# A decoder layer on one core: first weights ahead of the first activations, batched squares, an earlier first norm, full-height gate rows and a split memory scaling

## The chip, the cores and the metric

The kernel runs on one core of a Trainium2 chip. A core has five engines, each with its own in-order instruction stream: TensorE (PE, matrix multiply; its weight loads are shown apart as PEld), VectorE (DVE), ScalarE (ACT), GpSimd (POOL) and SyncE (SP), which here only issues DMA transfers from main memory to on-chip memory. Engines wait for one another through semaphores, so a waiting instruction holds everything behind it on its engine. Matmul results go to PSUM, of which the kernel uses eight banks: four for the large products (named mm) and four for everything else (named ax).

The metric is the device time of one execution in microseconds, from the runs' own times. Over three runs the kernel before took 1468.85, 1471.32 and 1471.49 us, a median of 1471.32.

## The reference, cut to what matters

One inference step of one trunk layer. The prompt of 256 tokens and 8 sample tokens go through the same weights, so activations are 264 columns wide; the model width is 2048.

```python
def layer(x, ...):
    xn = rmsnorm(x, g_mix)
    z = xn @ w_in                       # all group inputs from one projection
    xr, conv_new = causal_conv(z[..., OFF_RGX:OFF_RGG], conv_buf, conv_w, conv_b)
    ...                                 # RG-LRU: gates from block_diag(xr), then a scan
    y_rg = rmsnorm(h_rg * jax.nn.gelu(z[..., OFF_RGG:OFF_Q]), g_rg_out)
    ...                                 # q, k, v; gate rows logi, logf (4 heads)
    h_ml, C_new, n_new, m_new = mlstm(q, k, v, logi, logf, C0, n0, m0)
    y_ml = rmsnorm(h_ml, g_ml_out) * jax.nn.sigmoid(z[..., OFF_O:OFF_I])
    x = x + jnp.concatenate([y_rg, y_ml], axis=-1) @ w_out
    xq = rmsnorm(x, g_xa) @ w_xa_q
    ...                                 # cross attention over 256 memory tokens
    x = x + o @ w_xa_o
    xf = rmsnorm(x, g_ffn)
    x = x + (jax.nn.silu(xf @ w_ffn_gate) * (xf @ w_ffn_up)) @ w_ffn_down

def mem_kv(mem, g_mem, w_k, w_v):
    mn = rmsnorm(mem, g_mem)            # memory keys and values
    ...
```

All inputs and weights are float32. The final result is one more RMSNorm of x.

## The kernel before, in words

Activations are kept with channels on the 128 partitions and tokens in the columns: 16 chunks of 128 channels, each 264 wide. A float32 product is made of three single-pass products (`mm3`): every operand is split into a high part, rounded to the matmul type, and a low part, the remainder; high times high, high times low and low times high are accumulated in one PSUM bank.

The layer's weights are a list of `steps`, called blocks below and numbered from 0. A block is a weight column group of 128 outputs: 16 chunks times three products, 48 matmuls of 128x264. Blocks 0 to 7 make the RG-LRU input, 8 the gate rows of the mLSTM, 9 to 16 its q and k, 17 to 24 its v, 25 to 32 the RG-LRU's output gate (rgg), 33 to 40 the mLSTM's output gate (o), 41 to 56 w_out; the query, memory, attention output and feed-forward blocks follow. Blocks 0 to 3 are different: their weights come in quarters of the channels, and the four outputs are accumulated side by side in banks ax, ax, ax and mm (`pe_first`), so that the first matmuls need only the first chunks of the input.

Each block's weights come as two halves of 128x1024 float32 (buffers `raw`, five of them, filled by SP's DMA queue). `split_half` makes the two parts of a half: ACT copies it to the matmul type (`w<-raw`), and DVE subtracts that from the raw half (`w<-raw,w`). The split weights have four buffers `w`, two blocks' worth: a half's ACT copy waits until PE has done the last matmul that reads the buffer's old contents. So on ACT and DVE the splits of a block stand in the queue at a fixed distance ahead of PE, and what stands behind a split on either engine waits with it.

The order of instructions on the five engines is set when the program is built, by a scheduler that places them by its own estimate of when each could start, under priorities the code gives (`tc.high_priority`, `tc.issue_after`, `in_order`). Work beside the main stream is written as generators (`side`) that are advanced between blocks; `yield STEP` in one moves its next piece to a later block.

The first RMSNorm's factor (`rstd`) is not applied before the products but to their results. The input's squares are summed over chunks (`sumsq` into `acc_x`), PE sums that over partitions (three matmuls against `ones`, the token sums), DVE makes the inverse square root in a chain of small instructions (tiles `c`), PE spreads it over partitions (`ident` against `c`), and only then can the results of blocks 0 and on be evacuated from their banks: "evacuation" is the DVE instruction that multiplies a bank by `rstd` and frees it.

`ml_gates` turns block 8's rows into the mLSTM's gates, on 4 partitions, one for each head: it ends in nine small products that spread the rows over the partitions (tile ax to `bcs`, `gcol`, `emc`). `rg_gen` is the RG-LRU: sigmoids, then a run of exponentials and square roots on ACT. `ml_heads` is the mLSTM by heads, and `ml_norm` its norm with 24 one-column matmuls against `ones`. `mem_gen` normalises the memory: sixteen chunks, each multiplied by its factor and then split.

Of the kernel before, what the change touches and what calls it, by code (L numbers as in the profile page):

```python
# [80 lines left out]
def layer_kernel(ctx: ExitStack, tc, xT, memT, vec, wrg, w_in, w_out, w_q, w_k, w_v, w_o,  # L81
# [120 lines left out]
    def split_first(i, h):  # L202
# [9 lines left out]
        splits[i, h] = (wh, wl)  # L212

    def wrows(w, i):

        w = w[:, WO: WO + 8 * N].rearrange("p (c n) -> p c n", n=N)
        return w[:, :, 0: P], w[:, :, P: 2 * P]
# [97 lines left out]

    warm(12)
    onesr = const.tile([P, P], F32R, name="onesr")
# [276 lines left out]
    def evac_if(ps):  # L594
        R = Arr(7)
        ml["R"] = R
        li, u, a, b = (R(j)[0:4] for j in range(4))
        act.activation(halves(a), unturn(ps[64:68, :N]), AF.Copy)
# [14 lines left out]
    def ml_gates():  # L613
# [32 lines left out]
        for h in range(H):  # L646
            pe.matmul(ps[:, h * 16: h * 16 + 16], ident[0:4, h: h + 1].to_broadcast([4, P]), x16,
                      start=True, stop=True)
        i4 = ident[0:4, 0:4]
        for j in range(2):  # L650
            pe.transpose(ps[:, 64 + 4 * j: 68 + 4 * j], g[:, j * P: j * P + P], i4)
        for j, w0 in enumerate(WIN):
            pe.transpose(ps[:, 72 + 4 * j: 76 + 4 * j], b[:, w0: w0 + P], i4)
        act.activation(bcs, ps[:, 0:64].rearrange("p (h j) -> p h j", j=16), AF.Copy)
# [30 lines left out]
    def ml_prompt():  # L685
# [11 lines left out]
        R = ml["R"]  # L697
        M = R(6)[0:4, :T]
        for h in range(H):
            sel = ident[0:4, h: h + 1].to_broadcast([4, P])  # L700
            bc = bank("ax")
# [186 lines left out]
    def proj(src, rhs, evac, cols=2048, n=N, need=()):  # L888

        def f(i):  # L890
            ps = bank()
            w = W(i)
            nch = cols // P
            for c in range(nch):
                mm3(ps[:, :n], w(c), rhs(c), c == 0, c == nch - 1)
            return ps
        steps.append((src, cols, f, evac, need))
# [49 lines left out]
    def norm_x():  # L947
        yield from rstd_from(acc_x, rstd, D)
# [29 lines left out]
    def mem_gen():  # L978
# [14 lines left out]
        for c in range(KC):  # L993
            x = raw(c)
            dve.tensor_mul(x, x, r)
            m = rm(c)
            split(m[:, :T], m[:, T:], x, V("g_mem", c))
            yield 0.7

    def ry(c):  # L1000
# [304 lines left out]

    load_x(sp, 0, 1)
    for c in range(4):
        load_first(0, c)
    for i in range(1, 3):
        for c in range(0, 4, 2):  # L1310
# [3 lines left out]
        if i == 1:  # L1314
            sp.dma_start(vecs[:, 16:], vec[:, 16:])
    with tc.high_priority(), in_order():
        act.dma_start(vecs[:, 0:16], vec[:, 0:16])
        load_x(act, 1, 2)
        load_x(act, 2, 4)
        act.activation(warm_act, ones[:, 0:1], AF.Square)  # L1320
        split_half(0, 0)
        split_half(0, 1)

    pend = []
    for i, (src, cols, pef, evf, need) in enumerate(steps):
        if i > 1:
            load_piece(i + LD - 1)
        if i == 5:
            finish(lambda: fn.done)
            st["rg"] = side(rg_gen(), 0)  # L1330
        for q in need:
            if q in st:
                finish(lambda: st[q].done)
        if i != 4:
            with tc.high_priority(300):
# [6 lines left out]
        if i + LS < len(steps) and steps[i + LS][1] > 1024:  # L1342
            split_half(i + LS, 1)
        ps = pef(i)
        if 1 <= i < 4:
            with tc.issue_after(st["split"].ins):
                for c in range(4 * i if i > 1 else 0, 4 * i + 4):
                    sumsq(acc_x, xres[:, c, :], c == 0)
        if i == 3:
            fn = side(norm_x(), -1)  # L1350
        if evf is not None:
# [126 lines left out]
```

## Time and profile before

| what | value |
|---|---|
| median of three runs | 1471.32 us |
| the profiled execution's own time | 1470.12 us |
| its span, first to last instruction | 1468.0 us |
| PE busy in the span | 1447.7 us (99%) |
| DVE busy | 1054.0 us (72%) |
| ACT busy | 783.7 us (53%) |
| POOL busy | 125.7 us (9%) |
| mean granted TensorE clock | 0.994 |
| moved by DMA | 326.01 MB, 222 GB/s on average |

The table's profile is one execution. Its span is 2.1 us shorter than its own time, and its time is 1.2 us below the median. PE works for 99% of the span, so only its idle gaps and the instructions on it are to be won or lost; the groups' table gives each group's busy time, the mean time of one instruction, and the idle time of the engine just before them with the engine that ended it. A row's matmul ends are modelled: a matmul is shown with 0.28 us, although the next starts 0.11 us after it, so rows that follow each other overlap.

### The profile page before, as it was taken

How to read it: one execution, taken by the hardware profiler on the slowest of the kernel's cores; microseconds unless marked ns; L12 is line 12 of the kernel's file. 1: busy time of each engine (PE TensorE's matmuls, PEld its weight loads, DVE VectorE, ACT ScalarE, POOL GpSimd, SP SyncE). 2: the span in 40 equal slices, each digit the busy share in tenths (PEclk: the TensorE clock that was granted, in tenths of full speed). 3: DMA queues.
4: the chain of work that ended last, by engine and by line, in shares of the span. 5: the costliest groups of instructions: out<-in, count | busy, mean ns of one | idle time of the engine just before them, and what ended most of it. 6: DMA issues, size and time to landing. Idle time of an engine off the chain costs nothing.

```text
span 1468.0 us, 30204 instructions
## 1 busy us (share of the span) xinstructions
PE 1447.7 (99%) x12098; PEld 1423.3 (97%) x12098; DVE 1054.0 (72%) x2050; ACT 783.7 (53%) x1257; POOL 125.7 (9%) x190
## 2 busy tenths in 40 slices
PE   9999999999999999999999999999999999999997
PEld 9998899999999999999999999999999999999997
DVE  7986988798699999986666656555565655556564
ACT  7574775675455666665554444434444443444463
POOL 0001210000124344320000000000000000000000
PEclk9999999999999999999999999999999999999999
DMA  9555986556799979855555555555555555555563
GB/s 294 205 173 173 299 297 235 178 184 220 258 339 334 345 276 348 346 205 184 194 190 195 199 191 199 194 194 197 192 199 193 197 198 191 198 194 198 172 189 115
DMA packets 99756, 326.01 MB, mean 222 GB/s; under 512 B 10944, under 2 KB 19824, under 8 KB 99616
## 3 DMA queue, kind: packets, MB, share of 16 engines
q1 hardware_dynamic: 83472, 269.57, 53.8%
q0 software_dynamic: 15136, 53.16, 10.2%
q8 instruction: 94, 1.54, 0.4%
q10 hardware_dynamic: 1008, 1.36, 0.3%
q14 instruction: 46, 0.38, 0.1%
HBM read 312.78 MB, written 11.28 MB: 221 GB/s over the span
## 4 chain that ended last, share of the span: by engine, by line
PE 68%; DVE 1%; issue 0%; ACT 0%; POOL 0%; DVEq 0%; POOLq 0%; ACTq 0%
PE mm L60 65%; PE ax L60 2%; DVE B L60 0%; DVE w L60 0%; DVE dw L60 0%; POOL ds L1054 0%; ACT w L60 0%; DVE c L60 0%; ACT dw L60 0%; ACT ds L60 0%; DVE osm L60 0%; DVEq L1455 0%; ACT t L60 0%; DVE xres L60 0%; ACT c L60 0%
## 5 line engine op out<-in xcount | busy, mean ns | idle before, releaser
L60 PE MATMUL mm<-B,w 128*128 128x264 f32 (+1 forms) x10960 | 1285.7, 280 | 7.5 <-DVE w L60 3.6
L60 PEld LDWEIGHTS mm<-B,w 128*128 128x128 f32 x10960 | 1264.5, 190 | 15.7 <-DVE w L60 4.6
L60 DVE TENSOR_TENSOR w<-raw,w 128x1024 fp32r<-128x1024 f32 (+1 forms) x522 | 626.0, 1201 | 309.8 <-ACT w L60 309.1
L60 ACT ACTIVATE w<-raw 128x1024 fp32r<-128x1024 f32 (+1 forms) x522 | 535.7, 1028 | 539.5 <-PE mm L60 364.8
L60 PE MATMUL mm<-w,B 128*128 128x512 f32 x384 | 86.5, 380 | 0.0
L60 PEld LDWEIGHTS mm<-w,B 128*128 128x128 f32 x384 | 70.8, 190 | 9.3
L1370 POOL TENSOR_TENSOR B<-B,rstd 128x264 f32<-128x264 f32 x4 | 2.8, 743 | 803.7 <-ACT rstd L60 803.7
L60 DVE TENSOR_TENSOR t<-mm,rstd 128x264 f32<-128x264 f32 x104 | 44.9, 433 | 29.4 <-PE mm L60 29.4
L60 DVE SCALAR_TENSOR_TENSOR B<-B,dw 128x256 f32<-128x256 f32 x128 | 53.7, 474 | 2.9 <-ACT dw L60 2.7
L60 DVE TENSOR_TENSOR xres<-xres,mm 128x264 f32<-128x264 f32 (+1 forms) x81 | 34.4, 425 | 28.2 <-PE mm L60 28.1
L60 PE MATMUL ax<-B,B 128*128 128x256 f32 (+3 forms) x288 | 47.0, 304 | 1.8 <-DVE B L60 1.8
L60 DVE SCALAR_TENSOR_TENSOR dw<-B,qsm,dw 128x256 f32<-128x256 f32 x96 | 48.1, 509 | 0.7
L1054 POOL TENSOR_TENSOR ds<-dw,ds 128x256 fp32r<-128x256 f32 x32 | 35.9, 1122 | 106.0 <-ACT ds L60 105.9
L60 PEld LDWEIGHTS ax<-B,B 128*128 128x128 f32 x288 | 39.5, 191 | 5.3 <-DVE B L60 2.4
L60 ACT ACTIVATE B<-xres,vecs 128x264 fp32r<-128x264 f32 (+1 forms) x64 | 32.1, 501 | 2.5 <-DVE xres L60 2.0
L60 ACT ACTIVATE t<-xres 128x264 f32<-128x264 f32 (+1 forms) x61 | 23.9, 408 | 15.9 <-DVE xres L60 15.9
L1043 POOL DMA_DIRECT2D B<-kcT x32 | 17.3, 542 | 136.7 <-DVE B L60 123.6
L60 ACT ACTIVATE dw<-B,qsm 128x256 f32<-128x256 f32 x32 | 16.2, 507 | 21.5 <-issue 10.3
L60 ACT ACTIVATE t<-t 128x264 f32<-128x264 f32 (+1 forms) x61 | 24.8, 407 | 2.6 <-DVE t L60 2.6
L60 DVE TENSOR_TENSOR acc_x<-acc_x,t 128x264 f32<-128x264 f32 x59 | 25.3, 429 | 1.0 <-ACT t L60 0.5
L60 ACT ACTIVATE t<-B,B 128x128 f32<-128x128 f32 x64 | 21.6, 389 | 8.2 <-DMA B<-scr 8.2
L60 DVE SCALAR_TENSOR_TENSOR B<-xres,vecs,B 128x264 fp32r<-128x264 f32 x48 | 23.6, 491 | 3.1 <-ACT B L60 3.1
(152 smaller groups left out, 674.5 us busy)
## 6 DMA issues: line engine op xcount, KB each, us to landing
raw<-w_gu SPq DMA_DIRECT2D x176, 512.0 KB, 4.0
raw<-w_d SPq DMA_DIRECT2D x80, 512.0 KB, 4.3
raw<-w_in SPq DMA_DIRECT2D x74, 512.0 KB, 4.8
raw<-w_out SPq DMA_DIRECT2D x32, 512.0 KB, 4.3
B<-kcT POOLq DMA_DIRECT2D x32, 512.0 KB, 8.3
raw<-w_q SPq DMA_DIRECT2D x32, 512.0 KB, 4.2
B<-vcT POOLq DMA_DIRECT2D x32, 512.0 KB, 9.8
raw<-w_k SPq DMA_DIRECT2D x32, 512.0 KB, 5.4
```

Of the source, the lines that this page charges most:

```text
L60: return f(*a, **k)
L1043: pool_e.dma_start(kc, kcT[h, b])
L1054: pool_e.tensor_sub(ws[:, 1], acc, ws[:, 0].bitcast(F32))
L1370: e.tensor_mul(st["y"](c), st["y"](c), r)
```

## The change

The change has five parts.

Head: SP's first transfer is the first quarter of block 0's weights instead of the first input chunk; that chunk is issued by ACT ahead of the first vectors, and the other three of the first four by SP between the weights. The warm-up matmuls against `ones` go from 12 to 8 (each is two instructions in the profile).

Squares: the sixteen squares of single chunks are gone. After block 3, `first_squares` squares four chunks at a time on ACT (1056 columns), and DVE adds the four together and folds the sum to 264 columns.

First norm: the token sums are run inside block 5, after its first 8 chunks, and the spread inside block 6, after its first 4; PE's order is held as written from block 4 to block 6. The results of blocks 0 to 5 are handed to evacuation after that.

Gate rows: the two 4-row tiles that the small products read are cleared to 128 partitions, and the products are made over all 128, the five transposes as plain products with the identity.

Memory: the scaling of the memory chunks moves to a later block after every second chunk.

```diff
+    def first_squares():
+
+        a, b = (B([P, BW])[:, 0: 4 * N] for _ in range(2))
+        x = lambda q: xres[:, 4 * q: 4 * q + 4, :].rearrange("p c n -> p (c n)")
+        act.activation(a, x(0), AF.Square)
+        for q in range(1, 4):
+            act.activation(b, x(q), AF.Square)
+            dve.tensor_add(a, a, b)
+        dve.tensor_add(a[:, 0: 2 * N], a[:, 0: 2 * N], a[:, 2 * N:])
+        dve.tensor_add(acc_x, a[:, 0: N], a[:, N: 2 * N])
...
-    warm(12)
+    warm(8)
...
         ml["R"] = R
+        for q in range(2):
+            pool_e.memset(R.tile(q), 0.0)
...
         for h in range(H):
-            pe.matmul(ps[:, h * 16: h * 16 + 16], ident[0:4, h: h + 1].to_broadcast([4, P]), x16,
+            pe.matmul(ps[:, h * 16: h * 16 + 16], ident[:, h: h + 1].to_broadcast([P, P]), R(2)[:, 0:16],
                       start=True, stop=True)
-        i4 = ident[0:4, 0:4]
-        for j in range(2):
-            pe.transpose(ps[:, 64 + 4 * j: 68 + 4 * j], g[:, j * P: j * P + P], i4)
-        for j, w0 in enumerate(WIN):
-            pe.transpose(ps[:, 72 + 4 * j: 76 + 4 * j], b[:, w0: w0 + P], i4)
+        for o, x, at in ((64, R(5), WIN[:2]), (72, R(4), WIN)):
+            for j, w0 in enumerate(at):
+                pe.matmul(ps[:, o + 4 * j: o + 4 * j + 4], x[:, w0: w0 + P], ident[:, 0:4], start=True, stop=True)
...
-        M = R(6)[0:4, :T]
+        M = R(6)[:, :T]
         for h in range(H):
-            sel = ident[0:4, h: h + 1].to_broadcast([4, P])
+            sel = ident[:, h: h + 1].to_broadcast([P, P])
...
             for c in range(nch):
+                if (i, c) in ((5, 8), (6, 4)):
+                    with tc.high_priority():
+                        st["rstd_x"].run(lambda: True)
                 mm3(ps[:, :n], w(c), rhs(c), c == 0, c == nch - 1)
...
             split(m[:, :T], m[:, T:], x, V("g_mem", c))
             yield 0.7
+            if c % 2:
+                yield STEP
...
-    load_x(sp, 0, 1)
     for c in range(4):
         load_first(0, c)
+        if c == 0:
+            load_x(sp, 1, 2)
+        elif c == 1:
+            load_x(sp, 2, 4)
...
     with tc.high_priority(), in_order():
+        load_x(act, 0, 1)
         act.dma_start(vecs[:, 0:16], vec[:, 0:16])
-        load_x(act, 1, 2)
-        load_x(act, 2, 4)
...
+    kept = ExitStack()
...
-        if i == 5:
-            finish(lambda: fn.done)
+        if i == 6:
             st["rg"] = side(rg_gen(), 0)
...
-        if i != 4:
+        if not 4 <= i < 7:
...
+        if i == 4:
+            kept.enter_context(tc.manual_schedule(engines={mybir.EngineType.PE}))
         ps = pef(i)
-        if 1 <= i < 4:
-            with tc.issue_after(st["split"].ins):
-                for c in range(4 * i if i > 1 else 0, 4 * i + 4):
-                    sumsq(acc_x, xres[:, c, :], c == 0)
+        if i == 6:
+            kept.close()
         if i == 3:
-            fn = side(norm_x(), -1)
+            with tc.issue_after(st["split"].ins), tc.high_priority():
+                first_squares()
+            st["rstd_x"] = Gen(norm_x())
```

The diff says little of the order that comes out. In the rows below a tile's number tells instances apart and differs between the two programs.

Around the token sums, on PE in the program before (mm_633 is block 5, whose halves are w_533 and w_536; ax_513 takes the token sums):

```order
L60 MATMUL mm_633<-B_256,w_536 128x264
L60 MATMUL mm_633<-B_257,w_536 128x264
L60 MATMUL mm_633<-B_256,w_536 128x264 x2
L60 MATMUL mm_633<-B_257,w_536 128x264
L60 MATMUL ax_513<-ones,acc_x 128x1 x3
```

They stood five matmuls into the second half. The same place now (mm_541 is block 5, w_474 and w_477 its halves):

```order
L60 MATMUL mm_541<-B_170,w_474 128x264 x2
L60 MATMUL mm_541<-B_171,w_474 128x264
L60 MATMUL mm_541<-B_170,w_474 128x264
L60 MATMUL ax_566<-ones,acc_x 128x1 x3
L60 MATMUL mm_541<-B_252,w_477 128x264
```

They follow the last matmul of the block's first half at once. On DVE before, the last sums of squares stood between the splits of blocks 5 (w_533, w_536) and 6 (w_627, w_630):

```order
L60 TENSOR_TENSOR acc_x<-acc_x,t_500 128x264
L60 TENSOR_TENSOR w_536<-raw_441,w_536 128x8x128
L60 TENSOR_SCALAR t_697<-t_693 128x8
L60 TENSOR_TENSOR acc_x<-acc_x,t_503 128x264
L60 TENSOR_TENSOR w_627<-raw_509,w_627 128x8x128
L60 RECIPROCAL t_697<-t_697 128x8
L60 TENSOR_TENSOR acc_x<-acc_x,t_506 128x264
```

On DVE now (w_474 and w_477 are block 5's halves, w_535 and w_538 block 6's, w_614 the first half of block 7; B_459 and B_460 hold the squares):

```order
L60 TENSOR_TENSOR w_474<-raw_401,w_474 128x8x128
L60 TENSOR_TENSOR w_477<-raw_403,w_477 128x8x128
L60 TENSOR_TENSOR B_459<-B_459,B_460 128x1056
L60 TENSOR_TENSOR w_535<-raw_470,w_535 128x8x128
L60 TENSOR_TENSOR B_459<-B_459,B_460 128x1056
L60 TENSOR_TENSOR w_538<-raw_472,w_538 128x8x128
L60 TENSOR_TENSOR B_459<-B_459 128x528
L60 TENSOR_TENSOR w_614<-raw_531,w_614 128x8x128
L60 TENSOR_TENSOR acc_x<-B_459 128x264
```

The last fold now stands behind the split of a half that is two blocks ahead, w_614, which takes the buffer of w_474.

At the turn from rgg to o blocks, on DVE before (mm_2746 is an rgg block, t_2832 its evacuation; w_3006, w_3009 are the halves of block mm_3102, which is the next to take mm_2746's bank):

```order
L60 TENSOR_TENSOR w_3006<-raw_2894,w_3006 128x8x128
L60 TENSOR_TENSOR acc_rg<-acc_rg,t_2737 128x264
L60 SCALAR_TENSOR_TENSOR B_2612<-B_2612,bcs,t_2799 128x256
L60 SCALAR_TENSOR_TENSOR t_2803,nums<-B_2612,B_2613 128x128 x2
L60 TENSOR_TENSOR w_3009<-raw_2896,w_3009 128x8x128
L60 TENSOR_TENSOR B_2807<-B_2807,t_2811 128x264
L60 TENSOR_TENSOR B_2807<-B_2807,t_2817 128x264
L60 TENSOR_TENSOR B_2807<-B_2807,t_2823 128x264
L60 TENSOR_TENSOR t_2832<-mm_2746,rstd 128x264
```

On DVE now (mm_2742 is the rgg block, t_2831 its evacuation; block mm_3110, with halves w_3003 and w_3006, is the next to take its bank; w_3104 and w_3107 are the halves of the block after that):

```order
L60 TENSOR_TENSOR w_3006<-raw_2895,w_3006 128x8x128
L60 SCALAR_TENSOR_TENSOR B_2710<-B_2710,bcs,t_2810 128x256
L60 SCALAR_TENSOR_TENSOR t_2814,nums<-B_2710,B_2711 128x128 x2
L60 TENSOR_TENSOR w_3104<-raw_2992,w_3104 128x8x128
L60 SCALAR_TENSOR_TENSOR B_2710<-B_2710,bcs,t_2817 128x256
L60 SCALAR_TENSOR_TENSOR t_2821,nums<-B_2710,B_2711 128x128 x2
L60 TENSOR_TENSOR w_3107<-raw_2994,w_3107 128x8x128
L60 SCALAR_TENSOR_TENSOR B_2710<-B_2710,bcs,t_2824 128x256
L60 SCALAR_TENSOR_TENSOR t_2828,nums<-B_2710,B_2711 128x128
L60 TENSOR_TENSOR t_2831<-mm_2742,rstd 128x264
```

The evacuation now stands behind the splits of one block more. The buffer of w_3107 is that of the second half of block mm_3009, which PE runs just ahead of mm_3110.

In the memory's scaling, on DVE before (B_4205 to B_4212 hold two chunks each, so B_4209 to B_4212 are the second eight; w_4391 and w_4464 are halves of successive blocks):

```order
L60 TENSOR_TENSOR w_4391<-raw_4294,w_4391 128x8x128
L60 SCALAR_TENSOR_TENSOR B_4209<-B_3803,vecs,B_4209 128x256 x2
L60 SCALAR_TENSOR_TENSOR B_4210<-B_3803,vecs,B_4210 128x256 x2
L60 SCALAR_TENSOR_TENSOR B_4211<-B_3805,vecs,B_4211 128x256 x2
L60 SCALAR_TENSOR_TENSOR B_4212<-B_3805,vecs,B_4212 128x256
L60 TENSOR_TENSOR xres<-xres,mm_4394 128x264
L60 SCALAR_TENSOR_TENSOR B_4212<-B_3805,vecs,B_4212 128x256
L60 TENSOR_TENSOR w_4464<-raw_4369,w_4464 128x8x128
```

On DVE now (the corresponding splits are w_4406, w_4409 and w_4477, the second eight chunks are B_4175 to B_4178):

```order
L60 TENSOR_TENSOR w_4406<-raw_4317,w_4406 128x8x128
L60 TENSOR_TENSOR xres<-xres,mm_4339 128x264
L60 SCALAR_TENSOR_TENSOR B_4102<-xres,vecs,B_4101 128x264
L60 TENSOR_TENSOR acc_x<-acc_x,t_4330 128x264
L60 TENSOR_TENSOR w_4409<-raw_4319,w_4409 128x8x128
L60 TENSOR_TENSOR w_4477<-raw_4388,w_4477 128x8x128
L60 SCALAR_TENSOR_TENSOR B_4400<-xres,vecs,B_4399 128x264
L60 TENSOR_TENSOR acc_x<-acc_x,t_4403 128x264
L60 TENSOR_TENSOR xres<-xres,mm_4412 128x264
L60 SCALAR_TENSOR_TENSOR B_4175<-B_3769,vecs,B_4175 128x256 x2
```

The last eight scalings now follow the split w_4477 instead of preceding it; the first eight stand where they stood. The nine small gate products, which stood scattered over the last matmuls of block 17 and the first of block 18 in 13 instructions, now stand in one piece of 18 instructions ahead of block 16; the RG-LRU's run of exponentials and square roots on ACT stands ahead of the splits of block 19 instead of block 17.

## The prediction

> **What bounds the kernel now.** I read the page's engine shares and chain first, then the groups, then the stretches where PE stands still. The page:
>
> ```profile
> PE 1447.7 (99%) x12098; PEld 1423.3 (97%) x12098; DVE 1054.0 (72%) x2050; ACT 783.7 (53%) x1257; POOL 125.7 (9%) x190
> PE 68%; DVE 1%; issue 0%; ACT 0%; POOL 0%; DVEq 0%; POOLq 0%; ACTq 0%
> L60 PE MATMUL mm<-B,w 128*128 128x264 f32 (+1 forms) x10960 | 1285.7, 280 | 7.5 <-DVE w L60 3.6
> L60 DVE TENSOR_TENSOR w<-raw,w 128x1024 fp32r<-128x1024 f32 (+1 forms) x522 | 626.0, 1201 | 309.8 <-ACT w L60 309.1
> L60 ACT ACTIVATE w<-raw 128x1024 fp32r<-128x1024 f32 (+1 forms) x522 | 535.7, 1028 | 539.5 <-PE mm L60 364.8
> ```
>
> PE is busy for 99% of the span and carries 68% of the chain that ended last. The matmul group waits 7.5 us in all, most of it for weight splits. DVE (72%) and ACT (53%) have room, so work taken off them counts only where PE waits for that very work. Three prices decide: PE's step, the granted clock, and the stalls. Windows of the run, with length, PE busy and instructions, PEld, DVE, ACT, POOL, then the granted clock:
>
> ```profile
> 28.00:60.00 32.00, 29.52 (x257) 29.06 (x255) 28.45 (x92) 15.88 (x33) 0.00 (x0) 1.00 0.65 220
> 116.00:124.00 8.00, 6.88 (x35) 6.32 (x35) 8.00 (x13) 3.77 (x8) 0.00 (x0) 0.57 0.36 114
> 225.00:229.00 4.00, 4.00 (x23) 4.00 (x23) 3.88 (x15) 1.96 (x5) 0.00 (x0) 0.60 1.03 398
> 229.00:240.00 11.00, 11.00 (x99) 11.00 (x98) 8.44 (x20) 4.07 (x6) 0.00 (x0) 0.99 0.59 223
> ```
>
> The last row gives the step: 99 matmuls in 11.00 us, 0.111 us each at full clock, so a block of 48 takes 5.3 us. The two in the middle show a cost that no stall row names: the clock fell to 0.57 and 0.60. The loss is 8.00 x 0.43 = 3.4 us and 4.00 x 0.40 = 1.6 us. I price one dip at 1.7 us, half of the first. The first row held a stall of 2.0 us and kept 1.00.
>
> **The head.** PE's warm-up and first matmul, ACT's first work, and the issues on the queues of SP and ACT:
>
> ```profile
> 0.80 0.42 ACTq L1317 DMA_DIRECT2D vecs<-vec  x1
> 0.81 0.40 SPq L1304 DMA_DIRECT2D xres<-xT  x1
> 1.25 2.66 SPq L199 DMA_DIRECT2D raw<-w_in  x4
> 1.12 5.49 PE L60 MATMUL mm<-ones 128*128 128x128 f32 x24 [1.12 <-DVE ones L60]
> 3.62 0.50 ACT L60 ACTIVATE B<-xres,vecs 128x264 fp32r<-128x264 f32 x1
> 6.71 0.63 ACT L60 ACTIVATE w<-raw 128x512 fp32r<-128x512 f32 x1 [2.60 <-DMA raw<-w_in]
> 7.39 0.94 PE L60 MATMUL ax<-B,w 128*128 128x264 f32 x6 [0.78 <-ACT w L60]
> ```
>
> ACT had its first input chunk at 3.62 and then waited 2.60 us for the first weights, issued at 1.25 and usable at 6.71, that is 5.46 later. Issued first, at 0.81, they come 0.44 earlier if the 5.46 stands. The other end: the input chunk came in time for 3.62 after an issue at 0.81, 2.8 us for half the bytes; twice that is 5.6, no better, but issued alone the weights may take some 4 us, which is 1.9 earlier. I take 1.2, the middle. The chunk and the vectors now go out on ACT, one issue of 0.4 us more ahead of the chunk; both are ready at 3.62 with 2.6 to spare, so they hide. The other input chunks move between the weights on SP, each at 0.4 us to 0.66 us of issue; they are needed a chunk later each and PE then takes 48 matmuls a quarter, so I cost them at nothing; should they come late the gain shrinks. Eight warm-up pairs end near 1.12 + 5.49 x 8/12 = 4.8, which only leaves a gap ahead of about 6.0. **Head: -1.2** (ends -1.9 and, if the gap costs a dip, +0.5).
>
> **Squares and first norm.** PE, ACT and DVE around blocks 4 to 7:
>
> ```profile
> 28.53 0.28 PE L60 MATMUL mm<-B,w 128*128 128x264 f32 x1
> 29.94 6.23 PE L60 MATMUL mm<-B,w 128*128 128x264 f32 x53 [0.46 <-DVE w L60]
> 46.24 0.73 PE L60 MATMUL ax<-ident,c 128*128 128x128 f32 x6
> 47.01 0.39 ACT L60 ACTIVATE rstd<-ax 128x264 f32<-128x264 f32 x1 [2.18 <-PE ax L60]
> 47.43 1.51 DVE L60 TENSOR_TENSOR B<-ax,rstd 128x132 f32<-128x132 f32 x9 [1.88 <-ACT rstd L60]
> 48.85 0.56 DVE L60 TENSOR_TENSOR B<-mm,rstd 128x132 f32<-128x132 f32 x3
> 49.55 1.14 PE L60 MATMUL mm<-B,w 128*128 128x264 f32 x8 [2.03 <-DVE B L60]
> ```
>
> A lone matmul is shown with 0.28 us and the next starts 0.11 after it, so each stall costs 0.17 more than its idle time. Block 4 waited 0.46 for a DVE subtraction queued behind additions of squares; these now come behind the splits, so the stall goes: **-0.6**. The fifteen single additions and squares become three wide additions, two folds and four wide squares, about the same work, on DVE between the splits.
>
> Block 7 waited 2.03 for its bank: spread at 46.24, rstd at 47.01, twelve evacuating multiplications from 47.43, done when PE goes on at 49.55. From the spread's end, 46.97, that is 2.6 us. The spread now stands 12 matmuls into block 6, so 36 matmuls, 4.0 us, lie between. The stall goes: **-2.2**. What is late next is the token sum itself. It stands right behind the 24th matmul of block 5, and that matmul is the one that frees the buffer of w_614. On DVE the last fold into acc_x stands behind the subtraction for w_614, which needs ACT's copy, which needs that matmul. So PE stands still for the chain copy, subtraction, fold. Such rows, from the mLSTM's heads on DVE:
>
> ```profile
> 201.03 0.43 DVE L60 TENSOR_TENSOR t<-mm,rstd 128x264 f32<-128x264 f32 x1
> 207.65 1.22 DVE L60 TENSOR_TENSOR w<-raw,w 128x1024 fp32r<-128x1024 f32 x1
> 208.79 0.48 DVE L60 SCALAR_TENSOR_TENSOR B<-B,bcs,t 128x256 f32<-128x256 f32 x1
> 209.30 0.29 DVE L60 SCALAR_TENSOR_TENSOR t<-B,B 128x128 f32<-128x128 f32 x1
> ```
>
> The subtraction takes 1.14 to the next start, an addition 0.43; ACT's copy 1.03, from its group. With 0.04 at each of three handovers (46.97 to 47.01), 0.17 + 1.03 + 1.14 + 0.43 + 0.12 = 2.9 us. Behind it stand, on PE, the rest of block 5; on ACT and DVE nothing that PE needs sooner. Three wide additions, each about four of 0.43 less overhead, could leave DVE up to 0.7 late; I take **+3.1** (2.5 to 3.7). Then DVE's eleven small steps for the inverse root stand ahead of the next split, with 24 + 12 matmuls, 4.0 us, to cover them.
>
> **Gate rows.** The RG-LRU's run of exponentials and roots on ACT, before:
>
> ```profile
> 222.18 2.74 PE L60 MATMUL ax<-ones,B 128*128 128x1 f32 x24
> 113.59 1.04 ACT L60 ACTIVATE w<-raw 128x1024 fp32r<-128x1024 f32 x1
> 114.69 0.49 PE L60 MATMUL mm<-B,w 128*128 128x264 f32 x2 [1.86 <-ACT w L60]
> 115.11 0.84 PE L60 MATMUL ax<-B,ident 4*128 4x16 f32 x6
> 116.47 1.39 PE L60 MATMUL ax<-ident,B 4*128 4x4 f32 x6
> 118.98 7.23 PE L60 MATMUL mm<-B,w 128*128 128x264 f32 x43 [1.12 <-DVE w L60]
> ```
>
> The first row prices a small float32 matmul: 2.74 / 24 = 0.114 us. The gates' 13 instructions lay here inside the wait for ACT, so they were nearly free. Now 18 of them stand ahead of block 16 where PE does not wait: 18 x 0.114 = **+2.1**. The stalls, 1.86 and 1.12, end with ACT's run, which goes two blocks later unchanged, and so do they: 0, between -1.5 (fewer PE instructions inside) and +1.0. Two clears of 128x1056 on POOL, 9% busy, hide. Four more table loads on ACT in the rgg blocks fall where it is half idle: 0.
>
> **rgg to o blocks.** Because the heads' work comes two blocks later, the evacuation t_2831 stands on DVE behind the subtraction for w_3107, whose copy on ACT waits for the last matmul of the block that runs just ahead of mm_3110; and mm_3110 needs the bank which t_2831 frees. From those rows: 0.17 + copy 1.03 + subtraction 1.14 + scalar-tensor 0.51 and 0.22 (to the next starts; the second by its 0.29 less the overlap) + multiplication 0.43 + 0.12 = **+3.6** (3.0 to 4.2). Before, the evacuation in this place stood behind only that block's own splits, a block earlier, and PE shows no stall there.
>
> **Memory.** DVE ahead of the stall in the memory's scaling, and PE's waits in that stretch:
>
> ```profile
> 331.07 1.23 DVE L60 TENSOR_TENSOR w<-raw,w 128x1024 fp32r<-128x1024 f32 x1
> 332.20 2.87 DVE L60 SCALAR_TENSOR_TENSOR B<-B,vecs,B 128x256 fp32r<-128x256 f32 x7
> 335.71 1.23 DVE L60 TENSOR_TENSOR w<-raw,w 128x1024 fp32r<-128x1024 f32 x1
> PE mm L60 <- DVE w L60: 1.7, 1, 1.7
> ```
>
> Seven scalings of 2.87 us and one more held up the subtraction at 335.71. Now three splits come ahead of the last eight, so this stall goes: 1.67 + 0.17, **-1.8** (0 if the eight hold up the next split as much).
>
> **Sum.** -1.2 - 0.6 - 2.2 + 3.1 + 2.1 + 3.6 - 1.8 = +3.0. To it come dips: two waits of 3.1 and 3.6 are both longer than the 2.0 that kept the clock, and than the 1.86 and 1.12 that lost it with small matmuls between them. I take one dip, since where a wait falls decides: +1.7. Against the profiled execution's own 1470.12 (span 1468.0 plus 2.1 around it; 1.2 below the median) this gives 1470.12 + 4.7 = 1474.8 us.
>
> The Trainium skill ("TensorE: Matmul & The Clock Gate", Part 1 and "Why this matters for your kernels") says that the clock halves after an idle window of about 3.4 us, and that gaps above some 3 us are to be avoided. By that neither wait need cost a dip, and the sum would be 1473.1. The 2.0 us stall that kept 1.00 agrees; the row 116:124, where no gap reached 2 us, differs, and the measurement decides, so I keep one dip.
>
> **Rivals.** A: the waits come but no dip follows, 1470.12 + 3.0 = 1473.1, within 0.2% of the median. For it speaks the row 28:60, against it 116:124. By the rule of the Trainium skill above it would be so.
>
> B: both waits dip, 1476.5; for it speaks that 3.6 is longer than any stall shown.
>
> C, the other side: PE's 18 gate matmuls and the waits let ACT catch up, so that at the RG-LRU's run both stalls and their dip are gone: 1.86 + 1.12 + 0.34 + 3.4 = 6.7 us less, 1474.8 - 6.7 = 1468.1, faster than the median by 0.2%. It decides if ACT's split of 113.59 stands 3 us earlier against PE. Against it: ACT's copies wait for PE's buffers, so ACT cannot run ahead by more than the two blocks that it already has.
>
> D: the memory's or the head's part does not do what it says: the head late by the moved chunks, or the eight scalings stall the next split: 1474.8 + 1.8 = 1476.6.
>
> **How the numbers follow.** The measurement of this kernel cannot tell changes under about 0.2%, 2.9 us, from none: faster is below 1468.4, slower above 1474.3. Chances: the forecast with one dip 0.38, A 0.24, B 0.14, C 0.12, D 0.12. The forecast lies 0.5 above the bound, so of its 0.38 I count 0.08 as the same; A is the same, C is faster, B and D slower: faster 0.12, same 0.32, slower 0.56. The range runs from 1468.8, where A meets the head's and the gates' lower ends (1473.1 - 0.7 - 1.5 - the rest of the waits' ends, 1.2, = 1469.7, and a little toward C), to 1479.5: B with the upper ends of the head (+1.7) and the run (+1.0) is 1479.2.
>
> **What would show it.** In the changed profile: PE's first matmul near 6.2; no idle ahead of blocks 4 and 7; an idle of about 2.9 us ending with DVE's acc_x in block 5; 18 gate matmuls without idle around them; idle of about 3.4 us near 230 us, where block 33 begins, ended by t; no stall near 336; clock rows below 0.7 after one of the two waits. I am wrong if the two waits are under 1 us, or if the RG-LRU's stalls vanish.

## The result, and the profile after

The changed kernel is slower by 0.28%: a median of 1475.48 us (1471.83 to 1477.79, eight runs) against 1471.40 us for the kernel before on the same chip, ratio 1.0028 with a 95% interval of 1.0018 to 1.0038. On another chip, unaltered, it took 1472.61 against 1470.53 us, ratio 1.0021 (1.0007 to 1.0034). These ratios are worked out from all executions of both kernels, so they can differ a little from the ratio of the two medians. The forecast was 1474.8.

The profiled execution took 1475.16 us with a span of 1473.4, 5.4 more than before. PE's waits over the whole span (waiting line, releaser, us in total, times, longest):

```profile
PE ax L60 <- DVE B L60: 7.4, 4, 3.4
PE mm L60 <- DVE t L60: 3.6, 1, 3.6
PE mm L60 <- ACT w L60: 2.0, 1, 2.0
PE mm L60 <- DVE ones L60: 1.1, 1, 1.1
PE mm L60 <- DVE w L60: 1.1, 1, 1.1
PE ax L60 <- ACT w L60: 0.3, 1, 0.3
PE mm L60 <- DVE c L60: 0.3, 1, 0.3
```

Two of these are new and long: 3.4 us ended by DVE in block 5, and 3.6 us ended by t ahead of block 33. The waits for DVE's part of w, 3.6 us before, are down to 1.1. In the timeline of PE they stand here, with the new first matmul and the gate products:

```profile
5.21 1.69 PE L60 MATMUL ax<-B,w 128*128 128x264 f32 x6 [0.30 <-ACT w L60]
39.37 0.83 PE L60 MATMUL ax<-ones,acc_x 128*128 128x1 f32 x6 [3.40 <-DVE B L60]
90.14 1.05 PE L60 MATMUL ax<-B,B 128*128 128x264 f32 x4
90.83 5.76 PE L60 MATMUL mm<-B,w 128*128 128x264 f32 x48
103.61 0.96 PE L60 MATMUL ax<-B,ident 128*128 128x16 f32 x8
104.42 1.26 PE L60 MATMUL ax<-ident,B 128*128 128x4 f32 x10
178.64 2.93 PE L60 MATMUL ax<-B,B 128*128 128x256 f32 x8 [1.23 <-DVE B L60]
235.32 6.07 PE L60 MATMUL mm<-B,w 128*128 128x264 f32 x37 [3.57 <-DVE t L60]
```

Windows of PE behind them (length, PE busy and instructions, granted clock, DMA share, GB/s):

```profile
40.00:44.00 4.00, 4.00 (x24) 0.63 0.94 330
128.00:132.00 4.00, 2.13 (x10) 0.72 0.01 2
180.00:184.00 4.00, 4.00 (x18) 0.50 0.85 298
236.00:240.00 4.00, 4.00 (x25) 0.63 0.43 169
```

PE is fully busy in three of them, but runs 24, 18 and 25 instructions where 4 us at 0.111 us each would hold 36. The trace's clock record has, apart from one at the very end of both kernels, four stretches at half clock around and behind the waits, of 3.4, 6.8, 6.8 and 3.4 us from 41.0, 129.7, 177.5 and 235.6 us; before there were two, of 6.8 and 3.4 us from 116.5 and 225.8. Both traces have the same matmuls of split weights in the same order, so the start of a block's first one can be compared. After minus before, in us:

| start of block | changed kernel | e0_after (again) | what lies in between |
|---|---|---|---|
| 4 | -1.39 | -1.59 | head |
| 5 | -2.11 | -2.31 | block 4's stall gone |
| 6 | +3.22 | +2.80 | token sums' wait and half clock |
| 7 | +1.03 | +0.61 | its half clock ends; block 7's stall gone |
| 20 | +1.19 | +0.33 | gate products, RG-LRU's run |
| 33 | +2.95 | -0.66 | mLSTM's heads; wait ahead of block 33; the norm's sums and their half clock gone from here |
| 41 | +7.37 | +8.33 | half clock behind that wait, norm's sums |
| 57 | +5.43 | +6.39 | memory's stall gone |
| last matmul | +5.41 | +6.00 | |

### The profile page after: what moved, and what is told of

Same layout as the page of the kernel before. It is cut to its first block, busy times and chain, and to the rows that moved or that the text cites. A ratio compares the mean times of both kernels' runs of the same rounds, so it can differ in the third digit from the quotient of the medians.

```text
span 1473.4 us, 30180 instructions
## 1 busy us (share of the span) xinstructions
PE 1449.4 (98%) x12095; PEld 1426.9 (97%) x12095; DVE 1054.2 (72%) x2040; ACT 789.8 (54%) x1249; POOL 127.6 (9%) x192
## 4 chain that ended last, share of the span: by engine, by line
PE 67%; DVE 1%; issue 0%; ACT 0%; POOL 0%; DVEq 0%; POOLq 0%; ACTq 0%
PE mm L60 65%; PE ax L60 2%; DVE B L60 0%; DVE w L60 0%; DVE dw L60 0%; POOL ds L1070 0%; ACT w L60 0%; DVE c L60 0%; ACT dw L60 0%; ACT ds L60 0%; DVE osm L60 0%; DVEq L1475 0%; ACT t L60 0%; DVE xres L60 0%; ACT c L60 0%
## 5 line engine op out<-in xcount | busy, mean ns | idle before, releaser
L60 ACT ACTIVATE t<-xres 128x264 f32<-128x264 f32 (+1 forms) x46 | 18.7, 409 | 15.9 <-DVE xres L60 15.9
L60 ACT ACTIVATE B<-t 128x264 fp32r<-128x264 f32 (+1 forms) x60 | 24.1, 408 | 1.8 <-DVE t L60 1.8
```

What stands on the lines that cost most here:

```text
L60: return f(*a, **k)
```

## The experiments

Each is the changed kernel with one edit unless said otherwise. Where two kernels ran on different chips, their ratios to the kernel before are compared.

**The changed kernel again (e0_after).**

> The changed kernel once more, unaltered. Theory: the idle times that its order sets come back as they were (about 3.4 us ahead of the token sums, 2.0 and 1.1 at the RG-LRU's run, 3.6 ahead of block 33), while the stretches at half clock behind them may differ from the first profile's 41.0, 129.7, 177.5 and 235.6 us. Rival: the idle times themselves vary by more than 0.5 us from one execution to the next.

PE's waits of this execution:

```profile
PE ax L60 <- DVE B L60: 7.1, 4, 3.2
PE mm L60 <- DVE t L60: 3.6, 1, 3.6
PE mm L60 <- ACT w L60: 2.0, 1, 2.0
```

The long waits come back within 0.2 us. (In two of the kernels below whose order up to there is the same, e4_mem and e6_evac, the token sums waited 4.2 and 4.1 us, so they can also vary by a microsecond, and the rival has that much right.) The half clock comes back behind the token sums' wait and at the RG-LRU's run, but otherwise it differs: none near 178 us, 6.8 us instead of 3.4 around the end of block 33's wait, and another 6.8 us from 241.1 us on. Over its twelve executions, 1469.51 to 1479.66 us, span and mean granted clock go together (from 0.994 with 1467.8 to 0.988 with 1478.0; correlation -0.98). A clock lower by 0.006 over 1470 us is 8.8 us of the 10.2 between the two spans. So the order fixes where PE waits, and most of the scatter of this kernel goes with the time at half clock.

**Filling the token sums' wait (e1_fill).**

```diff
         ps = bank("ax")
+        for _ in range(fill):
+            pe.matmul(ps[:, :P], ones, ones, start=True, stop=True)
         token_sums(ps, acc)
...
-            st["rstd_x"] = Gen(norm_x())
+            st["rstd_x"] = Gen(norm_x(12))
```

> Twelve idle products of ones with ones (24 PE instructions) stand ahead of the token sums, in their bank, so that PE works while it would wait; nothing else moves. Theory: the wait is set by the chain copy, subtraction, fold on ACT and DVE, so the token sums start where they did (39.4 us); at 0.115 each the 24 instructions fill 2.75 of the 3.4 us, the clock dip of 3.4 us behind the wait goes, and the kernel is 1.7 us shorter than the changed one (some 1473.8). Rival: the dip does not come from the wait, it stays, and the time is the changed kernel's, 1475.5.

PE's timeline in this kernel, and its window behind:

```profile
35.86 2.84 PE L60 MATMUL ax<-ones 128*128 128x128 f32 x24
39.62 0.83 PE L60 MATMUL ax<-ones,acc_x 128*128 128x1 f32 x6 [0.92 <-DVE B L60]
```

```profile
40.00:44.00 4.00, 4.00 (x38) 1.00 0.89 305
```

The sums start 0.25 us later than without the filling, and the clock stays at 1.00 where it was 0.63. From block 5 to block 6 the changed kernel lost 5.33 us, this one 3.87: the 1.5 us between them, of the expected 1.7, are the half clock's. The ratio to before is 1.0012 (0.9997 to 1.0026), against 1.0021 and 1.0028; the theory holds in the profile, though by time alone the gain is not clear of zero. The dip behind this wait is paid in addition to it.

**The fold ahead of the split (e5_fold).** DVE's order from block 4 to 6 is held as written, and the squares are emitted behind block 5's splits:

```diff
-            kept.enter_context(tc.manual_schedule(engines={mybir.EngineType.PE}))
+            kept.enter_context(tc.manual_schedule(engines={mybir.EngineType.PE, mybir.EngineType.DVE}))
+            with tc.issue_after(st["split"].ins), tc.high_priority():
+                first_squares()
...
-            with tc.issue_after(st["split"].ins), tc.high_priority():
-                first_squares()
```

> DVE's order from block 4 to block 6 is held as written, with the squares' additions behind the splits of block 5, so that the last fold stands ahead of the split of block 7 that waits for PE. Theory: the idle of 3.4 us ahead of the token sums and its clock dip go, 3.6 + 1.7 = 5.3 us, less up to 0.8 for a short wait at the spread or at block 7: 1470.2 to 1471.0. Rival: DVE is so far behind with the wide additions that the sums wait all the same, at least half of the idle stays, 1473 or more.

DVE's timeline in this kernel:

```profile
32.48 1.26 DVE L60 TENSOR_TENSOR B<-B,B 128x1056 f32<-128x1056 f32 x1 [0.72 <-ACT B L60]
34.88 1.26 DVE L60 TENSOR_TENSOR B<-B,B 128x1056 f32<-128x1056 f32 x1 [1.15 <-ACT B L60]
37.29 1.26 DVE L60 TENSOR_TENSOR B<-B,B 128x1056 f32<-128x1056 f32 x1 [1.15 <-ACT B L60]
39.33 0.43 DVE L60 TENSOR_TENSOR acc_x<-B 128x264 f32<-128x264 f32 x1
```

The fold no longer stands behind the split of block 7, and PE waits 3.5 us all the same (3.53 against 3.40). My theory falls: the fold ahead of the split does not remove the wait. But the edit does two things. It also moves the squares a block later, so that the first wide addition starts at 32.48 us instead of 28.97, and DVE then waits twice for ACT's next square (1.15 us each), because squares and additions alternate through one buffer. How long the wait would be with the fold alone moved, this run does not show. Its ratio, 1.0008 (0.9995 to 1.0021), comes from a wait no shorter, so it is no gain of this edit.

**Single squares again (e8_single).**

```diff
         ps = pef(i)
+        if 1 <= i < 4:
+            with tc.issue_after(st["split"].ins):
+                for c in range(4 * i if i > 1 else 0, 4 * i + 4):
+                    sumsq(acc_x, xres[:, c, :], c == 0)
...
-            with tc.issue_after(st["split"].ins), tc.high_priority():
-                first_squares()
```

> The squares are taken one chunk at a time in blocks 1 to 3 again, as before; the early token sums and spread stay. Theory: the wait ahead of the token sums came from the wide additions, which keep DVE busy until 37.8 us, and from the fold behind a split; with the sums ready when PE arrives, 3.4 us of idle and the dip behind it go, 5.3 us in all, and up to 0.7 comes back ahead of block 4: 4.6 us shorter than the changed kernel on the same chip. Rival: the wait is the split's alone; the additions for the first chunks then delay block 4 and half of the idle stays, 2 us shorter at most.

DVE's last addition of squares in this kernel, and PE's token sums:

```profile
36.26 0.43 DVE L60 TENSOR_TENSOR acc_x<-acc_x,t 128x264 f32<-128x264 f32 x1
```

```profile
29.80 8.14 PE L60 MATMUL mm<-B,w 128*128 128x264 f32 x70 [0.73 <-DVE w L60]
37.78 0.72 PE L60 MATMUL ax<-ones,acc_x 128*128 128x1 f32 x6
```

The sums are ready 1.1 us before PE asks, the wait and its half clock are gone, and block 4's stall is back with 0.73. The time is 1469.92 us against e0_after's 1472.61 on the same chip, 2.7 shorter where 4.6 was expected, and level with the kernel before (0.9999, 0.9987 to 1.0010). In the profile block 6 starts 2.95 us earlier than in e0_after; the head's lead is partly lost, 0.42 instead of 1.59 us at block 4, because ACT and DVE have the single squares to do there. So it was the squares' part of the change that made the early norm wait. That part both batches them and starts them behind block 3; this run takes back both, so it does not tell them apart.

**The head of before (e2_head).**

```diff
-    warm(8)
+    warm(12)
...
+    load_x(sp, 0, 1)
     for c in range(4):
         load_first(0, c)
-        if c == 0:
-            load_x(sp, 1, 2)
-        elif c == 1:
-            load_x(sp, 2, 4)
...
-        load_x(act, 0, 1)
         act.dma_start(vecs[:, 0:16], vec[:, 0:16])
+        load_x(act, 1, 2)
+        load_x(act, 2, 4)
```

> The changed kernel with the head of before: first input chunk first on SP, the other chunks on ACT, twelve warm-up products. Theory: the first matmul is back at 7.4 us instead of 5.2, and since the first block then runs at full pace from its start, the end of block 3 comes 1.4 us later than in the changed kernel; the time is longer by that, some 1.4 us. Rival: the transfers bound the first blocks in both, the end of block 3 stays within 0.4 us, and so does the time.

PE's token sums and DVE's fold in this kernel:

```profile
38.85 0.83 PE L60 MATMUL ax<-ones,acc_x 128*128 128x1 f32 x6 [1.25 <-DVE acc_x L60]
```

```profile
38.36 0.43 DVE L60 TENSOR_TENSOR acc_x<-B 128x264 f32<-128x264 f32 x1
```

Block 4 starts 0.24 us later than in the kernel before, so the new head is worth 1.6 us up to there, as the theory has it. But the sums are ready at almost the same moment (38.8 against 39.3 us), PE waits 1.25 instead of 3.40, no half clock follows, and block 6 starts 2.2 us earlier than in the changed kernel. The ratio is 1.0013 (1.0001 to 1.0025), no worse than the changed kernel's, so the 1.4 us do not reach the time. In these profiles what the new head gains is spent waiting for the squares. The scheduler also put the fold ahead of the split here, so the 2.2 us are not the head's alone.

**Gate rows on 4 partitions (e3_gates).**

```diff
-        for q in range(2):
-            pool_e.memset(R.tile(q), 0.0)
...
-            pe.matmul(ps[:, h * 16: h * 16 + 16], ident[:, h: h + 1].to_broadcast([P, P]), R(2)[:, 0:16],
+            pe.matmul(ps[:, h * 16: h * 16 + 16], ident[0:4, h: h + 1].to_broadcast([4, P]), x16,
...
-        for o, x, at in ((64, R(5), WIN[:2]), (72, R(4), WIN)):
-            for j, w0 in enumerate(at):
-                pe.matmul(ps[:, o + 4 * j: o + 4 * j + 4], x[:, w0: w0 + P], ident[:, 0:4], start=True, stop=True)
+        i4 = ident[0:4, 0:4]
+        for j in range(2):
+            pe.transpose(ps[:, 64 + 4 * j: 68 + 4 * j], g[:, j * P: j * P + P], i4)
+        for j, w0 in enumerate(WIN):
+            pe.transpose(ps[:, 72 + 4 * j: 76 + 4 * j], b[:, w0: w0 + P], i4)
...
-        M = R(6)[:, :T]
+        M = R(6)[0:4, :T]
...
-            sel = ident[:, h: h + 1].to_broadcast([P, P])
+            sel = ident[0:4, h: h + 1].to_broadcast([4, P])
```

> The gate rows are put back on 4 partitions (products and transposes as before); the place on PE stays ahead of block 16. Theory: the 2.1 us belong to the place, not to the partitions, so only the 5 instructions fewer count: 0.6 us shorter than the changed kernel, some 1474.9. Rival: the 128 partitions themselves cost the 2.1 us, 1473.4.

The products stay ahead of block 16, and the stretch around them is 0.5 us shorter than in the changed kernel, from the start of block 9 to that of block 17. The theory holds: the width costs 0.5 us, the place the rest. The ratio is 1.0016 (1.0005 to 1.0028). This kernel shows something else. PE at block 33, and the windows around:

```profile
230.62 4.29 PE L60 MATMUL mm<-B,w 128*128 128x264 f32 x36 [3.57 <-DVE t L60]
```

```profile
228.00:232.00 4.00, 1.38 (x12) 1.00 0.65 236
232.00:236.00 4.00, 4.00 (x39) 1.00 0.37 146
```

The same wait of 3.57 us, to the hundredth, kept the full clock here. The Trainium skill's page "TensorE: Matmul & The Clock Gate", Part 1, says that the activity window of about 3.4 us is free-running and that the clock is halved after at least one idle window. The runs agree that a wait's length alone does not decide: 3.57 us cost no clock here and 3.4 us at half clock in the changed kernel. They do not bear out that a whole window must be idle: a wait of 3.2 us lost the clock in e0_after, and 1.74 and 1.23 us, with four small matmuls and two of a block between them, were followed by 6.8 us at half clock in the changed kernel.

**Another buffer for the rgg results (e6_evac).**

```diff
     def evac_rgg(n):
         def f(ps):
-            z = tmp()
+            z = ltmp()
```

> The result tile of the rgg evacuation comes from the pool lt instead of t, which the heads use; that lets the evacuations stand ahead of the splits of later blocks. Theory: the wait ahead of block 33 (3.57 us shown) and the dip behind it go, but the 24 one-column sums then lie as they did before the change and may cost their own dip of 1.7: 3.7 to 5.4 us shorter than the changed kernel, 1470.1 to 1471.8. Rival: the heads are late altogether and the idle turns up at another block, 1474 or more.

PE's timeline in this kernel where the norm's sums begin:

```profile
227.83 12.09 PE L60 MATMUL mm<-B,w 128*128 128x264 f32 x106
240.79 4.02 PE L60 MATMUL ax<-ones,B 128*128 128x1 f32 x24 [0.88 <-DVE B L60]
```

The wait of 3.57 us is gone: from block 32 to block 33 this kernel gains 1.7 us on the one before, and the changed kernel loses 2.1. So the evacuations were late because their tile shared a ring of buffers with the heads' tiles. A wait of 0.88 us appears at the norm's sums instead, and 6.8 us of half clock begin within them, at 242.2 us (the 24 one-column matmuls take 4.02 us, against 2.74 at full clock in the kernel before). The ratio, 1.0016 (1.0005 to 1.0027), is less of a gain than the 3.7 us or more expected.

**Memory in one run (e4_mem).**

```diff
             yield 0.7
-            if c % 2:
-                yield STEP
```

> The memory's scaling is put back into one run of sixteen chunks; nothing else moves. Theory: the idle of 1.7 us near 336 us comes back, 1.9 us longer than the changed kernel on the same chip. Rival: the earlier shift of work by two blocks had already removed it, and the time is the same.

PE's waits between 300 and 360 us in this kernel:

```profile
PE mm L60 <- DVE w L60: 1.7, 1, 1.7
```

The stall is back, and with it 1.94 us between blocks 49 and 57. So the theory holds in the profile. The times cannot tell the two kernels apart: the median, 1473.67 us, is 1.1 more than e0_after's on the same chip, but the ratios to before, 1.0023 (1.0008 to 1.0038) and 1.0021, are almost equal.

**The three edits together (e7_best), and with the old head (e9_head).** e7_best has the edits of e8_single, e6_evac and e3_gates; e9_head is e7_best with e2_head's edit.

> The changed kernel with three edits: single squares as in e8_single, rgg results from pool lt as in e6_evac, gate rows on 4 partitions as in e3_gates. Theory: 4.6 + 3.7 + 0.5 = 8.8 us shorter than the changed kernel, so some 3 to 4 us shorter than the kernel before. Rival: without the waits the heads wait for DVE instead, and it is within 1.5 us of the kernel before.

> e7_best with the head of before. In e7_best the first matmul came at 5.1 us, but ACT then waited 4.9 us in the first blocks for weights, and the end of block 3 was 1.4 us later than in the kernel before. Theory: with the single squares in blocks 1 to 3 the new head gains nothing, since PE meets the waits for weights that it would have met later; with the old head the end of block 3 is within 0.5 us of the kernel before, and the time equals e7_best's within 1 us. Rival: the transfers' times merely scattered in that one execution; the new head is worth its 1.4 us here too, and e9_head is 1.4 us longer than e7_best.

| kernel | median, us | before, same chip | ratio (95% interval) |
|---|---|---|---|
| e7_best | 1466.76 | 1470.53 | 0.9978 (0.9967 to 0.9989) |
| e9_head | 1466.63 | 1471.38 | 0.9969 (0.9957 to 0.9981) |

Both beat the kernel before, by 0.22% and 0.31%. e7_best is 5.9 us below e0_after where 8.8 was expected. By its ratio e9_head is not slower than e7_best: its first matmul comes at 7.2 us, yet its block 4 starts 0.2 us earlier than in the kernel before, while e7_best's starts 1.4 later. With the single squares the new head brings nothing that these runs show.

## Why the prediction came out right

The time is 0.7 us from the forecast, and the sum's +4.7 stands against +5.0 in the profiled executions' own times. The terms, as predicted and as measured from block to block:

| term | predicted | measured |
|---|---|---|
| head | -1.2 | -1.4 |
| block 4's stall | -0.6 | -0.7 |
| block 7's stall | -2.2 | -2.2 |
| token sums' wait | +3.1 | +3.6 (3.40 shown, 0.17 to add) |
| gate products, at their new place | +2.1 | +2.2 |
| RG-LRU's run | 0 (-1.5 to +1.0) | -0.7 |
| wait ahead of block 33 | +3.6 | +3.7 (3.57 shown, 0.17 to add) |
| memory's stall | -1.8 | -1.9 |
| half clock, net | +1.7 | +4.8 |

The gate products' 2.2 us are the 2.90 lost around block 16's start less 0.69 for RG-LRU products that moved in between (four records, 90.14 to 90.83 in PE's timeline above). From the start of block 17 to that of block 20 the change is -1.5 us, of which 0.8 are nine small products that moved behind block 20; the other 0.7 is the RG-LRU's row. There the 13 gate products left the run, and PE's waits in it went from 3.3 to 4.1 us. So the products had not been quite as free in their old place as the prediction took them to be.

The half clock's row counts, for the matmuls that start in these stretches, their steps (from start to start, less idle time) beyond the mean step of the same matmuls at full clock: 9.4 us after, 4.6 before. As a check, 20.5 us at half clock after and 10.2 before bound the difference at 5.1.

The rows add up to +7.4, against +5.4 measured at the last matmul. What is missing lies for the most part between blocks 20 and 41, where the change is +6.2 us: idle time gives +4.2 (6.5 us instead of 2.3), the half clock +3.2, the nine moved products +0.8, and shorter steps of other matmuls, most of them small products, -2.0. Why these steps are shorter stays open.

The places and the signs are as forecast, and so are the sizes, to 0.5 us, of every row but those of the RG-LRU's run and the half clock. That the total came out within 0.3 us in the executions' own times is in part luck: the half clock cost 3 us more than the forecast allowed, and the RG-LRU's run and the shorter steps took most of that back. Single executions also scatter by more than this (10 us over e0_after's twelve).

Head: right in size, not in form. The first matmul came at 5.21 us instead of near 6.2, but six matmuls then took 1.69 us instead of 0.94, and block 1 already stood at -1.39. The prediction had not counted these slower first matmuls, so here too the size is partly luck.

Token sums: the place and nearly the length were as forecast, but not the chain that ended last. ACT's copy and DVE in the changed kernel:

```profile
36.01 1.06 ACT L60 ACTIVATE w<-raw 128x1024 fp32r<-128x1024 f32 x1 [0.28 <-PE mm L60]
```

```profile
28.97 1.26 DVE L60 TENSOR_TENSOR B<-B,B 128x1056 f32<-128x1056 f32 x1 [0.72 <-ACT B L60]
34.82 1.26 DVE L60 TENSOR_TENSOR B<-B,B 128x1056 f32<-128x1056 f32 x1
35.99 1.22 DVE L60 TENSOR_TENSOR w<-raw,w 128x1024 fp32r<-128x1024 f32 x1
37.13 0.70 DVE L60 TENSOR_TENSOR B<-B 128x528 f32<-128x528 f32 x1
37.75 1.22 DVE L60 TENSOR_TENSOR w<-raw,w 128x1024 fp32r<-128x1024 f32 x1
38.88 0.43 DVE L60 TENSOR_TENSOR acc_x<-B 128x264 f32<-128x264 f32 x1
```

The copy ended at 37.07, as the forecast chain has it, yet DVE took the subtraction up at 37.75 only, 0.68 later: it had no pause from the first wide addition on. The prediction had allowed "up to 0.7 late" and took 0.2 of it. But it took the chain through the copy as the one that ends last, and the runs show that DVE's own queue is. In all six kernels with this order on DVE (the changed kernel, e0_after, e1_fill, e3_gates, e4_mem, e6_evac) it works without a pause for 10.34 us from the start of the first wide addition to the end of the fold, and the token sums follow 0.06 later. The first wide addition starts between 28.55 us (e0_after) and 30.76 (e6_evac), and the sums move with it. Ahead of it ACT's copies wait for weights, 0.67 us in the changed kernel and 1.78 in e6_evac, so the moment when weights arrive moves the sums too.

Had the last fold followed the one at 37.13 directly, it would have ended near 38.3, still 2.3 us after PE's last matmul at 35.97. So the fold's place behind the split is worth about 1.0 of the 3.4 us. Earlier additions alone would bring about 0.7, because the chain through the copy then ends last. These two figures are worked out from the rows; no run changes one alone. e8_single, in which both go, shows that the wait then goes altogether.

Gate rows: the cost at the new place was right (18 instructions, and e3_gates' 0.5 us for five fewer); what the old place gives back was within the prediction's range for the RG-LRU's run, but taken at nothing.

Block 33 was right, as a chain too. ACT and DVE ahead of its first matmul, which starts at 235.32:

```profile
231.78 1.06 ACT L60 ACTIVATE w<-raw 128x1024 fp32r<-128x1024 f32 x1 [1.05 <-PE mm L60]
```

```profile
232.88 1.23 DVE L60 TENSOR_TENSOR w<-raw,w 128x1024 fp32r<-128x1024 f32 x1 [0.41 <-ACT w L60]
234.02 0.48 DVE L60 SCALAR_TENSOR_TENSOR B<-B,bcs,t 128x256 f32<-128x256 f32 x1
234.53 0.29 DVE L60 SCALAR_TENSOR_TENSOR t<-B,B 128x128 f32<-128x128 f32 x1
234.75 0.43 DVE L60 TENSOR_TENSOR t<-mm,rstd 128x264 f32<-128x264 f32 x1
```

Copy, subtraction, two heads' instructions and the evacuation follow each other as forecast. e6_evac removes the wait by the evacuation's buffer alone, which the prediction had not named as the reason for its place.

Heads: the prediction has no term for them. Before, they waited here:

```profile
155.59 0.92 PE L60 MATMUL ax<-B,B 128*128 128x256 f32 x4 [0.62 <-DVE B L60]
163.87 0.66 PE L60 MATMUL ax<-ident,B 128*128 128x128 f32 x4 [0.49 <-DVE B L60]
165.69 1.57 PE L60 MATMUL ax<-B,B 128*128 128x256 f32 x8 [1.16 <-DVE B L60]
```

These waits became 1.74 and 1.23 us, and 6.8 us of half clock followed in the profiled execution. Ahead of the first of them DVE waited for a store of results:

```profile
175.73 0.74 DVE L60 TENSOR_SCALAR B<-ax,gcol 128x256 f32<-128x256 f32 x2 [0.67 <-DMA o_sc<-B]
```

e0_after, with the same order, had no half clock there and started block 33 at -0.66 instead of +2.95. So the order alone does not fix this loss. It is not the profiled execution's alone either: e1_fill and e6_evac have 3.4 and 6.8 us at half clock in the same place.

Half clock: one dip more than before was taken as likeliest; two came, and the stretch behind the heads was not foreseen at all. The token sums' wait lost the clock in all six profiles in which it was 3.2 us or longer, and in none of the five in which it was 1.25 or shorter. Block 33's wait, 3.57 or 3.58 us in eight profiles, lost it in six. The rivals: A (no dip) did not happen in the profiled execution nor in e0_after, where both waits have a stretch at half clock; e3_gates and e2_head show that block 33's wait can pass without one. B (both waits dip) happened in the profiled execution, with the one-column sums' dip gone in exchange; in e0_after, e1_fill, e5_fold and e8_single there is one behind these sums again. C (the RG-LRU's stalls vanish) did not happen: 2.0 and 1.1 us of waits for w and 6.8 us of half clock, as before. D did not either; the memory's stall went.

## What to carry to other kernels

Work that is batched and moved behind a stage leaves the time where the engine was idle for the time where it is behind; check where the first user of its result will stand before calling it the same work. When two chains end at the same place, taking one away shows the other: here neither an earlier start of the matmuls nor the fold moved ahead of the split, with later squares, shortened the path while the additions were late. Tiles of unrelated work that share a ring of buffers also share their order, and a one-word change of pool took away a wait of 3.6 us.

## What the runs showed that was not expected

Executions of one kernel differ by up to 11.6 us (e4_mem). In e0_after, the changed kernel once more, span and granted clock go together, and between the profiles of these kernels it is the time at half clock that differs most: from 6.8 us in e2_head to 27.3 us in e6_evac. Block 33's wait was followed by none in two profiles, 3.4 us in three and 6.8 us in three. The 24 idle products of 2.84 us kept the clock at 1.00 through a wait that lost it in every profile in which it was left idle for 3.2 us or more.
